# Depthwise convolution by token pairs in one step of a streaming encoder

## The chip, the cores and the metric

The kernel runs on one core of a Trainium2 chip. The metric is the device time of one execution in microseconds (us). The kernel before takes 1048.87 us (median of 3 runs, 1048.4 to 1048.88).

## The reference

One layer of a streaming encoder: 16 meta tokens and 1024 prompt frames of a new stream, and 32 frames of a running stream. One input projection feeds two head groups. Group A is a gated linear unit (GLU), then a causal depthwise convolution of width 31 over 512 channels, a LayerNorm over the channels and a swish. Group B is sliding-window attention with sinks. Both go through one output projection; a convolutional feed-forward and norms follow.

```python
def conv_module(glu_ext, dw_w, dw_b, ln_g, ln_b):
    y = depthwise_causal_conv(glu_ext, dw_w, dw_b)      # y[t] = b + sum_k w[k] * glu_ext[t + k], k = 0..30
    return jax.nn.silu(layernorm(y, ln_g, ln_b))
...
        a_out = conv_module(glu_ext, conv_dw_w[l], conv_dw_b[l], conv_ln_g[l], conv_ln_b[l])
        attn = prompt_attention(q, k, v, rel_bias_table, attn_sinks[l])
        xp = xp + jnp.concatenate([a_out, attn], axis=-1) @ w_out[l]
        xp, ffn_state = conv_ffn(xp, ..., norm_ffn[l], w_up[l], ffn_dw_w[l], ffn_dw_b[l], w_down[l])
```

## The kernel before

Channels lie on the 128 partitions, tokens along the free dimension. Tokens come in three blocks of 336, 384 and 352 (`TB`). Every product of large matrices is three matmuls of rounded parts: each operand is split into a high part (a cast on ScalarE, ACT) and a low part (a subtraction on VectorE, DVE, or a negated copy on ScalarE plus an accumulating DMA on GpSimd's queue, POOL). `mm3` (L252) issues the three: high by high (L255), high by low (L256), low by high (L257). TensorE is PE in the profile.

The stages, in order of time: the input projection (to about 164 us, the last two of its columns within attention), attention (164 to 248 us), the output projection, first its attention half (248 to 293 us, tiles `cah`, `cal`), then its convolution half (from 293 us, tiles `cvh`, `cvl`), and the feed-forward (to 990 us and beyond).

The convolution is done on VectorE, one instruction per tap and piece (`conv_taps`, L395; taps at L400 for the first and L403 for the rest): `acc = glu * w + acc`, with one weight per partition. There are four blocks of 128 channels, p = 0 to 3. `SEGS` (L84) says in which pieces of tokens a block is done: block 0 in two, of which 20 taps of the long one are done by ScalarE and accumulating DMAs (`chain_taps`, L414); blocks 1 and 2 in one piece of 1090 columns; block 3 in three pieces of 324, 384 and 382. A piece can begin when the GLU of its last token block is there. Taps wait in a queue (`tapq`) as chains. `taps(us)` (L437) takes taps from the first two chains in turn until a budget is spent, counting (n + 120) / 960 us for n columns; they are given a very low priority.

The order on TensorE and ScalarE is written out by hand in this part (`manual_schedule`, L709): these engines run in program order. VectorE's, SyncE's and GpSimd's orders are fixed when the program is built, by a simulated time line, in which a ready instruction of higher priority goes first.

Attention is a loop of 20 steps (L1007). Step i does the scores, the row maximum (here a minimum of negated scores, L757, DVE) and the exponentials (L764, ACT) of job i; the scaling by the reciprocal of the sum and the transposes (L821, L823, PE; copied out at L828, ACT) of job i - 1; and the product with the values (L837, L841, PE) and its copy (L845, ACT) for job i - 2. `SCA[i]` (L73) is how many of up to four scalings ScalarE does (L774); VectorE does the rest (L772). Between, `FILL[i]` (L76) rows of the last two input columns give TensorE work until step 11; from step 13 `AH` (L86) rows of the output projection do. `TA[i]` (L55) is the budget of taps. `ca_split` (L931) splits the attention output; the parts named in `CSD` (L85) have their low part made by ScalarE and a DMA, the others by VectorE (L250).

After attention come 20 groups of the attention half, four rows of three matmuls each (L1118). Each row is followed by a `tick` (L1095), so there are 80 ticks. Ticks drive three LayerNorms (`ln`, L1050), one per token block: the first begins at tick `LN0` = 14, each next one at least `LNS` ticks later, and only when all taps of its token block are issued (`any(t[0] <= b for t in tapq)`). Within one, `LNW` (L67) spaces the parts: sums, mean on TensorE (L1059) and its subtraction (L1061), squares (L1065, L1067), the sum of squares on TensorE (L271), which stands 4 + 3 + 9 = 16 ticks after the beginning, the scale (L286, L292, L1077), the swish (L1080), and last the split into `cvh` and `cvl` (L249, L250). That split needs its buffers, which `open_cv` (L1108) opens in the place of the GLU once the sums of squares of all three are issued; the test stands at the end of a group (L1134). Ahead of each token block of the convolution half, what is left of its LayerNorm is run off, in program order.

The weights of the convolution half are four tiles, used in the order `WOC` = (0, 2, 1, 3), each for two of eight output rows i (`conv_half`, L1155). The first is split within the attention half, the other three right after it, one after the other (L1141): a cast on ScalarE (L240), a subtraction on VectorE (L242), then `fetch` starts the next load. Two load buffers (`raw`) are there, so that the fourth tile's load waits for the second's split.

Of the kernel before, what the change touches and what calls it, by code (L numbers as in the profile page):

```python
# [18 lines left out]
P = 128  # L19
# [32 lines left out]
NPB = 8  # L52
TGS = [3.0, 3.0, 1000.0, 1000.0]
TGW = [3.0, 5.0, 6.5, 3.5, 1000.0, 1000.0, 5.0, 1000.0, 1000.0, 1000.0, 3.5, 3.5, 1000.0, 1000.0, 1000.0, 1000.0, 1000.0, 1000.0, 3.0, 3.0, 1000.0, 1000.0, 1000.0, 1000.0, 1000.0, 1000.0, 7.0, 3.5, 3.5, 3.5]
TA = [2.01, 2.74, 5.63, 6.64, 4.22, 3.28, 2.42, 2.68, 2.08, 1.57, 2.08, 2.08, 3.18, 1.41, 2.1, 0.85, 4.71, 3.21, 5.98, 2.57]  # L55
TH = 5.9
WAYS = 2
BS = ((0, 2), (1, 0), (2, 1), (2, 2))
# [11 lines left out]
WLD = True  # L70
MANUAL = {mybir.EngineType.PE, mybir.EngineType.Activation}
MANEND = MANUAL | {mybir.EngineType.DVE}
SCA = [1, 2, 2, 2, 1, 1, 2, 2, 2, 2, 2, 1, 2, 2, 0, 1, 1, 2, 2, 2]  # L73
LN0 = 14
LNS = 21
FILL = [4, 6, 6, 2, 3, 3, 6, 1, 3, 3, 1, 4, 5, 0, 3, 6, 0, 3, 0, 3]  # L76
ORDER = [2, 3, 8, 9, 4, 5, 10, 11, 12, 13, 6, 7]
CHAINS = ((0, 1),)
# [2 lines left out]
CHK = 21  # L81
CHT = 0
CHG = (1, 2)
SEGS = (((0,), (1, 2)), ((0, 1, 2),), ((0, 1, 2),), ((0,), (1,), (2,)))  # L84
CSD = ['12', '00']  # L85
AH = (1, 2, 1, 3, 5, 4, 5)  # L86
AG = (('00', '02'), ('h',), ('l',), ('10',), ('12',))
AT = (1, 8)
# [81 lines left out]
def body(nc, tc, cp, wp, xp, dp, io):  # L170
# [221 lines left out]

    tapq, spare = [], [0.0, 0]

    def conv_taps(p, a0, a1, b):  # L395
        e, a = glu[:, p, :], acc[:, p, a0:a1]

        def tap(k):
            if k == 0:
                nc.vector.tensor_scalar(out=a, in0=e[:, a0:a1], scalar1=pcol("cw", p * CW), scalar2=pcol("cb", p),  # L400
                                        op0=ALU.mult, op1=ALU.add)
            else:
                nc.vector.scalar_tensor_tensor(out=a, in0=e[:, a0 + k:a1 + k], scalar=pcol("cw", p * CW + k),  # L403
                                               in1=a, op0=ALU.mult, op1=ALU.add)

        ks = list(range(CW))
        if (p, b) in CHAINS:
            ks = [0, *range(CHK, CW)]
            chq.append([p, a0, a1, list(range(1, CHK))])
        tapq.append([b, a1 - a0, tap, ks, p])  # L410
# [288 lines left out]
    def fetch():  # L699
        if wsrc:  # L700
            raws.append(wraw(wsrc.pop(0)))
# [434 lines left out]
    if not CVH:  # L1136
# [1 line left out]
        while len(squared) < 3:  # L1138
            tick()
        open_cv()  # L1140
    for m2 in WOC[1:]:  # L1141
        whl[m2] = halves(take((None, None, *wres)[m2], WLD))
        fetch()

    close(cS)
    cH, ph = pool("h3", "right")
# [8 lines left out]
    def conv_half(b, rms):  # L1155
        t0, n = OB[b]
        at = t0 - H0
        for i, m in enumerate(2 * h + j for h in WOC for j in range(2)):
            hi, lo = whl[m // 2][m % 2]
            ps = mmt()[:, :n]  # L1160
            for k in range(4):
# [736 lines left out]
```

## Time and profile before

| what | value |
| --- | --- |
| median of 3 runs | 1048.87 us |
| the profiled execution | 1049.94 us |
| its span, first to last instruction | 1048.2 us |
| granted TensorE clock | 0.999 of full |
| TensorE busy | 1030.8 us (98%) |
| VectorE busy | 864.8 us (83%) |
| ScalarE busy | 506.6 us (48%) |
| DMA, mean | 119 GB/s |

A row of a group gives the line, the engine, the operation, what is written and read, the shape and the count, then the busy time in us and the mean of one in ns, then the engine's idle time ahead of them. A row of the time line or of the chain begins with its start and its length in us from the start of the span. A row of a stage gives its bounds and length, the busy time of PE, PEld (weight loading), DVE, ACT and POOL with the numbers of instructions, the granted clock, the share of the DMA engines and GB/s. [...]

### The profile page before, as it was taken

The numbers are of one execution on the slowest core, as the hardware profiler recorded it, in microseconds if no ns is written. First come the engines' busy times: TensorE is split into PE (matmuls) and PEld (weight loads), VectorE is DVE, ScalarE is ACT, GpSimd is POOL, SyncE is SP. The second block draws the span as 40 slices with busy tenths as digits, with TensorE's granted clock in tenths as the row PEclk, the third lists the DMA queues.
The fourth block names the chain that finished last, engine by engine and source line by source line (L and its number), as shares of the span: only waits on it lengthen the run. The fifth ranks groups of instructions, "written<-read, shape, count | busy, mean of one in ns | idle before, by whom it ended". The sixth has DMA issues, their size and how long they took to land.

```text
span 1048.2 us, 19994 instructions
## 1 busy us (share of the span) xinstructions
PE 1030.8 (98%) x7747; PEld 1004.9 (96%) x7747; DVE 864.8 (83%) x1649; ACT 506.6 (48%) x1074; POOL 163.0 (16%) x205
## 2 busy tenths in 40 slices
PE   9999999989999999999999999999999999999997
PEld 8999998758999999999999999999999999999997
DVE  7999988899978978888887888888777976986636
ACT  8653336896676744433333443343336722532334
POOL 1133220002325220001000000110010041000043
PEclk9999999999999999999999999999999999999999
DMA  7378673124963123243233233332426795832204
GB/s 268 90 170 163 146 152 81 41 54 70 174 151 108 61 71 102 72 141 96 72 110 125 63 103 109 97 103 76 130 63 207 250 194 132 249 123 69 94 2 166
DMA packets 69047, 124.41 MB, mean 119 GB/s; under 512 B 10448, under 2 KB 42568, under 8 KB 68952
## 3 DMA queue, kind: packets, MB, share of 16 engines
q1 hardware_dynamic: 56392, 97.77, 29.2%
q0 software_dynamic: 12128, 24.95, 14.1%
q8 instruction: 61, 1.00, 0.4%
q10 hardware_dynamic: 432, 0.41, 0.1%
q14 instruction: 34, 0.28, 0.1%
HBM read 79.42 MB, written 27.51 MB: 102 GB/s over the span
## 4 chain that ended last, share of the span: by engine, by line
PE 88%; ACT 6%; DVE 3%; DMA 2%; issue 1%; DVEq 0%; ACTq 0%
PE mm L1282 55%; PE mm L255 10%; PE mm L256 10%; PE mm L257 10%; ACT pb L764 1%; DVE acc L403 1%; ACT glu L828 1%; DMA raw<-woc 1%; PE R L292 1%; ACT hi L341 1%; PE R L271 1%; DMA xs<-xT 0%; ACT glu L764 0%; ACT pb L774 0%; DMA prm<-prm 0%
## 5 line engine op out<-in xcount | busy, mean ns | idle before, releaser
L1282 PE MATMUL mm<-bh,sl 128*128 128x264 f32 (+1 forms) x912 | 214.0, 284 | 0.0
L1282 PEld LDWEIGHTS mm<-bh,sl 128*128 128x128 f32 x912 | 157.2, 188 | 0.0
L403 DVE SCALAR_TENSOR_TENSOR acc<-glu,prm,acc 128x324 f32<-128x324 f32 (+4 forms) x190 | 155.0, 844 | 1.1
L1282 PE MATMUL mm<-bl,sl 128*128 128x264 f32 (+1 forms) x424 | 120.9, 285 | 0.0
L1282 PE MATMUL mm<-th,rawr 128*128 128x264 f32 x640 | 120.0, 284 | 0.0
L1282 PE MATMUL mm<-bh,wlo 128*128 128x264 f32 (+1 forms) x440 | 117.6, 284 | 0.0
L1424 DVE TENSOR_TENSOR x<-x,mm 128x264 f32<-128x264 f32 (+7 forms) x238 | 76.5, 347 | 45.6 <-PE mm L1282 45.4
L1282 PE MATMUL mm<-bh,whi 128*128 128x264 f32 (+1 forms) x440 | 112.5, 284 | 0.0
L255 PE MATMUL mm<-hi,whi 128*128 128x352 f32 (+3 forms) x312 | 104.0, 333 | 0.0
L256 PE MATMUL mm<-lo,whi 128*128 128x352 f32 (+3 forms) x312 | 101.2, 324 | 0.2 <-DVE lo L342 0.2
L257 PE MATMUL mm<-hi,wlo 128*128 128x352 f32 (+3 forms) x312 | 101.2, 324 | 0.0
L1282 PEld LDWEIGHTS mm<-th,rawr 128*128 128x128 f32 x640 | 100.4, 188 | 0.0
L1282 PE MATMUL mm<-th,sl 128*128 128x264 f32 x352 | 92.7, 284 | 0.0
L1282 PE MATMUL mm<-tl,rawr 128*128 128x264 f32 x320 | 90.8, 284 | 0.0
L1282 PEld LDWEIGHTS mm<-bh,wlo 128*128 128x128 f32 x440 | 80.6, 188 | 0.0
L1282 PEld LDWEIGHTS mm<-bl,sl 128*128 128x128 f32 x424 | 79.9, 188 | 0.0
L1282 PEld LDWEIGHTS mm<-bh,whi 128*128 128x128 f32 x440 | 79.0, 188 | 0.0
L1282 PE MATMUL mm<-bl,whi 128*128 128x264 f32 (+1 forms) x272 | 77.5, 285 | 0.0
L1218 ACT CAST sl<-x 128x512 fp32r<-128x512 f32 (+1 forms) x41 | 29.7, 727 | 74.2 <-DMA x<-wup 41.0
L1282 PEld LDWEIGHTS mm<-th,sl 128*128 128x128 f32 x352 | 63.8, 188 | 0.0
L1282 PEld LDWEIGHTS mm<-tl,rawr 128*128 128x128 f32 x320 | 60.3, 188 | 0.0
L255 PEld LDWEIGHTS mm<-hi,whi 128*128 128x128 f32 x312 | 58.7, 188 | 1.2 <-issue 0.6
(400 smaller groups left out, 2923.1 us busy)
## 6 DMA issues: line engine op xcount, KB each, us to landing
x<-wup SPq DMA_DIRECT2D x20, 512.0 KB, 4.3
x<-wup SPq DMA_DIRECT2D x40, 256.0 KB, 2.8
yq<-x SPq DMA_DIRECT2D x32, 264.0 KB, 2.8
wlo<-raw POOLq DMA_DIRECT2D x16, 512.0 KB, 4.6
ca<-ca POOLq DMA_DIRECT2D x18, 383.0 KB, 5.2
raw<-win SPq DMA_DIRECT2D x12, 512.0 KB, 4.5
raw<-wdn SPq DMA_DIRECT2D x12, 512.0 KB, 4.6
rb<-yq SPq DMA_DIRECT2D x10, 528.0 KB, 5.0
```

Source lines behind the costliest of these rows:

```text
L255: nc.tensor.matmul(ps, whi(k), xhi(k), start=first and i == 0, stop=False)
L256: nc.tensor.matmul(ps, whi(k), xlo(k), start=False, stop=False)
L257: nc.tensor.matmul(ps, wlo(k), xhi(k), start=False, stop=last and i == n - 1)
L271: nc.tensor.matmul(ss[:, i:i + 1], z[:, at:at + P], ones[:, 0:1], start=j == 0, stop=j == len(parts) - 1)
L292: nc.tensor.matmul(R[:, at:at + P], left[i], diag[i], start=True, stop=True)
L341: hid[b, k] = nc.scalar.activation(HI[b][:, k, :], X[b][:, k, :], AF.Copy, scale=pcol("g1", k)).ins
L403: nc.vector.scalar_tensor_tensor(out=a, in0=e[:, a0 + k:a1 + k], scalar=pcol("cw", p * CW + k), in1=a, op0=ALU.mult, op1=ALU.add)
L764: nc.scalar.activation(qs_[i], qs_[i], AF.Exp, bias=m[0][:, i:i + 1], scale=-1.0, accum_out=m[1][:, i:i + 1])
L828: nc.scalar.copy(ptb[kv], pts[kv])
L1218: nc.scalar.copy(hi, raw)
L1282: nc.tensor.matmul(ps, w[:, j, :], x[:, j, :], start=first and j + i == 0, stop=j == 3 and i == 2, skip_group_check=True)
L1424: summed[0] = nc.vector.tensor_tensor(out=z, in0=z, in1=ps[:, lo_:hi_], op=ALU.add).ins
```

## The change

Block 1 and block 2 (whole) and block 3 (its two later token blocks as one piece now) are convolved by pairs of neighbouring output columns. With `y0`, `y1` the even and odd outputs, e(k) every second input from k on, and w the 31 weights, the sums e(1) + e(2) are made once (one instruction of n + 14 columns, kept where acc of block 3 or glu of block 2 is free). Fifteen taps with the odd weights go over shifted windows of these sums into `y1`, which then holds S = b + sum_j w[2j+1] (e(2j+1) + e(2j+2)). Then y0 = S + sum_j (w[2j] - w[2j-1]) e(2j) and y1 = S + sum_j (w[2j] - w[2j+1]) e(2j+1), sixteen taps each, in turn: three half sums of products where the direct form has four. So a piece of 2n columns takes 1 + 15 + 32 = 48 instructions of about n columns, where 31 of 2n columns stood. All operands but the sums are read and written at every second element. The weight differences are made once on GpSimd (`pdif`).

With it go: new budgets `TA` for steps 7 to 19 (fewer taps in 12 to 17); one scaling fewer on ScalarE in steps 12, 13 and 16 (`SCA`); no part of the attention output split by ScalarE and DMA (`CSD` empty), so that VectorE subtracts; `LNS` 24 for 21; and the fourth weight tile of the convolution half is split ahead of row 4 of the first token block instead of right behind the third's.

```diff
-TA = [2.01, 2.74, 5.63, 6.64, 4.22, 3.28, 2.42, 2.68, 2.08, 1.57, 2.08, 2.08, 3.18, 1.41, 2.1, 0.85, 4.71, 3.21, 5.98, 2.57]
+TA = [2.01, 2.74, 5.63, 6.64, 4.22, 3.28, 2.42, 2.7, 2.5, 2.3, 2.4, 2.4, 1.9, 0.9, 0.9, 0.9, 0.9, 0.9, 3.0, 3.0]
...
-SCA = [1, 2, 2, 2, 1, 1, 2, 2, 2, 2, 2, 1, 2, 2, 0, 1, 1, 2, 2, 2]
+SCA = [1, 2, 2, 2, 1, 1, 2, 2, 2, 2, 2, 1, 1, 1, 0, 1, 0, 1, 2, 2]
 LN0 = 14
-LNS = 21
+LNS = 24
...
-SEGS = (((0,), (1, 2)), ((0, 1, 2),), ((0, 1, 2),), ((0,), (1,), (2,)))
-CSD = ['12', '00']
+SEGS = (((0,), (1, 2)), ((0, 1, 2),), ((0, 1, 2),), ((0,), (1, 2)))
+PAIRS = ((1, 0), (2, 0), (3, 1))
+NP2 = CW // 2
+CSD = []
...
+    pdif = cp.tile([P, NCV - 1, 2, NP2], F32, tag="pdif", name="pdif")
+    co = PRM["cw"][0] + CW
+    wv = prm[:, co:co + (NCV - 1) * CW].rearrange("p (a b) -> p a b", b=CW)
+    nc.gpsimd.tensor_tensor(out=pdif[:, :, 0], in0=wv[:, :, 2::2], in1=wv[:, :, 1::2], op=ALU.subtract)
+    nc.gpsimd.tensor_tensor(out=pdif[:, :, 1], in0=wv[:, :, 0:CW - 1:2], in1=wv[:, :, 1::2], op=ALU.subtract)
+
+    def pair_place(p, n):
+        return (None, acc[:, 3, ACCW - n:], acc[:, 3, 0:n], glu[:, 2, 0:n])[p]
+
+    def pair_taps(p, a0, a1, b):
+        n = (a1 - a0) // 2
+        sums = pair_place(p, n + NP2 - 1)
+        y = [acc[:, p, a0 + i:a1:2] for i in range(2)]
+
+        def e(k, m=n):
+            return glu[:, p, a0 + k:a0 + k + 2 * m - 1:2]
+
+        def one(out, x, w, into):
+            nc.vector.scalar_tensor_tensor(out=out, in0=x, scalar=w, in1=into, op0=ALU.mult, op1=ALU.add)
+
+        def tap(k):
+            i, j = k
+            if i == 0:
...
+                nc.vector.tensor_tensor(out=sums, in0=e(1, m), in1=e(2, m), op=ALU.add)
+            elif i == 1:
+                w, x = pcol("cw", p * CW + 2 * j + 1), sums[:, j:j + n]
+                if j == 0:
+                    nc.vector.tensor_scalar(out=y[1], in0=x, scalar1=w, scalar2=pcol("cb", p), op0=ALU.mult,
+                                            op1=ALU.add)
+                else:
+                    one(y[1], x, w, y[1])
+            elif i == 2:
+                w = pcol("cw", p * CW) if j == 0 else pdif[:, p - 1, 0, j - 1:j]
+                one(y[0], e(2 * j), w, y[0] if j else y[1])
+            else:
+                w = pdif[:, p - 1, 1, j:j + 1] if j < NP2 else pcol("cw", p * CW + CW - 1)
+                one(y[1], e(2 * j + 1), w, y[1])
+
+        ks = [(0, 0), *((1, j) for j in range(NP2)), *((i, j) for j in range(NP2 + 1) for i in (2, 3))]
+        tapq.append([b, n, tap, ks, p])
+
     def conv_taps(p, a0, a1, b):
+        if (p, b) in PAIRS:
+            pair_taps(p, a0, a1, b)
+            return
...
-    for m2 in WOC[1:]:
+    def conv_weights(m2):
         whl[m2] = halves(take((None, None, *wres)[m2], WLD))
         fetch()
+
+    for m2 in WOC[1:3]:
+        conv_weights(m2)
...
         for i, m in enumerate(2 * h + j for h in WOC for j in range(2)):
+            if b == 0 and i == 4:
+                conv_weights(WOC[3])
```

More of the change, by code (lines that the diff above doesn't have):

```diff
@@ L393, in body @@
     tapq, spare = [], [0.0, 0]
+    pdif = cp.tile([P, NCV - 1, 2, NP2], F32, tag="pdif", name="pdif")
[16 more added lines that the diff above has]
+            if i == 0:
+                assert not any(q[4] == p - 1 and (p == 3 or len(q[3]) > 2 * (NP2 + 1)) for q in tapq if q[2] is not tap)
+                m = n + NP2 - 1
+                nc.vector.tensor_tensor(out=sums, in0=e(1, m), in1=e(2, m), op=ALU.add)
[14 more added lines that the diff above has]
+        tapq.append([b, n, tap, ks, p])
     def conv_taps(p, a0, a1, b):
+        if (p, b) in PAIRS:
+            pair_taps(p, a0, a1, b)
+            return
         e, a = glu[:, p, :], acc[:, p, a0:a1]
```

## The prediction

> **What bounds the kernel now.** I read the page first, then the busy time by stage, then TensorE's waits.
>
> ```profile
> span 1048.2 us, 19994 instructions
> PE 1030.8 (98%) x7747; PEld 1004.9 (96%) x7747; DVE 864.8 (83%) x1649; ACT 506.6 (48%) x1074; POOL 163.0 (16%) x205
> ```
>
> TensorE is the bound of the whole; a shorter vector program is worth only what TensorE idles for. The stages (start:end, length, busy time of PE, PEld, DVE, ACT, POOL) say where it idles. The input projection is the first row, attention steps 0 to 5 the second, steps 6 to 11 the third, 12 to 17 the fourth; then come the attention half of the output projection and, from 293 us, its convolution half.
>
> ```profile
> 42.00:164.00 122.00, 121.94 (x759) 119.27 (x757) 114.42 (x165) 50.47 (x86) 29.66 (x42) 1.00 0.71 149
> ...
> 164.00:193.00 29.00, 27.42 (x201) 22.23 (x199) 22.73 (x90) 23.91 (x82) 0.85 (x1) 1.00 0.26 60
> 193.00:216.00 23.00, 22.24 (x166) 16.82 (x166) 22.67 (x83) 19.05 (x65) 0.00 (x0) 1.00 0.05 19
> 216.00:244.00 28.00, 23.44 (x176) 16.44 (x178) 27.81 (x103) 27.38 (x88) 3.31 (x3) 1.00 0.34 65
> 244.00:294.00 50.00, 50.00 (x319) 48.14 (x314) 43.44 (x97) 33.32 (x72) 18.35 (x17) 1.00 0.73 127
> 294.00:312.00 18.00, 16.05 (x106) 15.55 (x105) 13.64 (x23) 11.13 (x23) 4.10 (x5) 1.00 0.66 180
> 312.00:990.00 678.00, 678.00 (x5456) 677.92 (x5455) 557.38 (x927) 284.89 (x538) 79.67 (x100) 1.00 0.39 117
> ```
>
> TensorE idles 1.58, 0.76 and 4.56 us in the attention stretches, and 1.95 from 294 us: 8.85 us, the most that this change can win. Its waits in steps 0 to 5, in steps 12 to 17 and from 294 us (engine, line, releaser: total, times, longest):
>
> ```profile
> PE pt L821 <- DVE glu L772: 1.0, 1, 1.0
> ...
> PE o L837 <- ACT ca L845: 2.2, 5, 0.8
> PE pt L821 <- ACT pb L774: 1.3, 2, 0.9
> PE o L902 <- ACT ca L845: 0.8, 1, 0.8
> ...
> PE mm L255 <- DVE x L1165: 1.9, 2, 1.7
> ```
>
> In steps 12 to 17 the releaser is ScalarE, and both ScalarE (27.38 of 28) and VectorE (27.81) are full. In steps 6 to 11 VectorE is full (22.67 of 23) and ScalarE is not, while TensorE has only 0.76 us to spare.
>
> **The pair arithmetic.** What one tap costs (line, engine, shapes, count, busy time, mean ns), and how close taps follow each other in the time line (start, length of the run):
>
> ```profile
> L403 DVE SCALAR_TENSOR_TENSOR acc<-glu,prm,acc 128x1090 f32<-128x1090 f32 x60 | 80.3, 1348 | 0.6
> L403 DVE SCALAR_TENSOR_TENSOR acc<-glu,prm,acc 128x324 f32<-128x324 f32 x55 | 30.1, 547 | 0.2
> L400 DVE TENSOR_SCALAR acc<-glu,prm 128x1090 f32<-128x1090 f32 x2 | 1.7, 841 | 0.0
> ...
> 193.66 2.33 DVE L403 SCALAR_TENSOR_TENSOR acc<-glu,prm,acc 128x324 f32<-128x324 f32 x4
> 244.34 4.83 DVE L403 SCALAR_TENSOR_TENSOR acc<-glu,prm,acc 128x384 f32<-128x384 f32 x9
> ```
>
> The first two rows give a line: (1348 - 547) / (1090 - 324) = 1.05 ns per element, so 778 ns at 545 elements and 609 at 383. Nine taps of alternating chains take 4.83 us, 0.54 each, 0.07 less than one alone: taps overlap by that much. So a tap takes 1.27 us at 1090, 0.70 at 545, 0.53 at 383, 0.47 at 324. Four taps of one chain on the same accumulator take 2.33, 0.58 each: a tap that needs the one before it costs 0.1 more.
>
> A channel block of 1090 columns costs 30 x 1.27 + 0.77 = 38.9 us now, and as pairs 48 instructions of 0.70, 33.6: 5.3 us less for each of blocks 1 and 2. Block 3's two long pieces cost 62 x 0.53 = 32.9 now and 48 x 0.53 = 25.4 as one pair: 7.5 less. Three sums for four save 18 us of VectorE, not a quarter of it, since 48 short instructions pay the fixed part where 31 paid it. The two weight differences are 45 elements each on POOL, which is idle for most of the span (163.0 us busy); I put them at nothing, since block 1's first tap, the first that could wait for them, is late enough (63.98 us, a row below).
>
> No instruction of this trace reads every second element, so 0.70 is an assumption: bounds are 0.70 (as 545 adjacent elements) and 1.27 (as if all 1090 were passed over). I take 0.70, because the instruction still reads and writes 545 elements.
>
> [...]
>
> **Steps 0 to 5.** Block 2's taps run into attention now:
>
> ```profile
> 63.98 0.84 DVE L400 TENSOR_SCALAR acc<-glu,prm 128x1090 f32<-128x1090 f32 x1
> ...
> 113.35 0.84 DVE L400 TENSOR_SCALAR acc<-glu,prm 128x1090 f32<-128x1090 f32 x1
> ...
> 165.19 1.34 DVE L403 SCALAR_TENSOR_TENSOR acc<-glu,prm,acc 128x1090 f32<-128x1090 f32 x1
> ...
> 173.74 1.34 DVE L403 SCALAR_TENSOR_TENSOR acc<-glu,prm,acc 128x1090 f32<-128x1090 f32 x1
> ```
>
> Blocks 1 and 2 begin at 63.98 and 113.35; the last two rows are the first and last of the five long taps after 164 us (6.4 us). VectorE is 114.42 of 122 us full before that, so of both savings (10.6 us) at least 7 arrive at the end of block 2, and the five vanish. The one wait on VectorE (L772, 1.0 us) goes: **-1.0 us** (0 if the pairs are late, -1.2 with its restart). The other waits there are ScalarE's and stay.
>
> **Steps 6 to 11.** Block 3's long piece can begin only when its last columns are there (the 216.12 row), so here only its first piece, 324 wide, runs, as one chain. The budgets of steps 7 to 11 rise from 10.49 to 12.3 us. Counting as the code does (444/960 us a tap of 324), 27 taps are issued in steps 6 to 11 before and 32 after. What ran:
>
> ```profile
> 216.12 0.55 DVE L582 SCALAR_TENSOR_TENSOR glu<-mm,glu 128x320 f32<-128x320 f32 x2
> ...
> L403 DVE SCALAR_TENSOR_TENSOR acc<-glu,prm,acc 128x324 f32<-128x324 f32 x18 | 9.9, 549 | 0.2
> L403 DVE SCALAR_TENSOR_TENSOR acc<-glu,prm,acc 128x384 f32<-128x384 f32 x7 | 4.3, 612 | 0.0
> ```
>
> These 25 and two first taps are the 27. Five more add 5 x 0.47 = 2.4; seven narrower ones take off 0.4; about half of them wait for their predecessor, +0.7. Of 2.7 us, TensorE's slack takes about 0.8: **+1.9 us** (0 if taps find gaps, +2.7 if no slack).
>
> **Steps 12 to 17.** Budgets fall from 15.46 to 6.4 us. VectorE gains three softmax scalings and four subtractions, ScalarE loses three scalings and four negated copies:
>
> ```profile
> L774 ACT ACTIVATE pb<-pb,sm 128x209 f32<-128x209 f32 x14 | 6.4, 487 | 0.0
> ...
> L936 ACT ACTIVATE cal<-ca 128x384 fp32r<-128x384 f32 x2 | 1.1, 560 | 0.0
> ...
> L936 ACT ACTIVATE cal<-ca 128x324 fp32r<-128x324 f32 x2 | 1.0, 476 | 0.0
> ...
> L772 DVE TENSOR_SCALAR pb<-pb,sm 128x209 f32<-128x209 f32 x10 | 3.0, 321 | 0.0
> ...
> L250 DVE TENSOR_TENSOR cvl<-acc,cvh 128x324 fp32r<-128x324 f32 x4 | 1.8, 490 | 0.0
> ```
>
> VectorE's balance is some -9.1 + 3 x 0.24 + 4 x 0.42 = -6.7 us (the last row is a subtraction of the same kind); ScalarE's 3 x 0.37 + 2 x 0.38 + 2 x 0.42 = 2.7 (each 0.1 less than its busy time, for overlap). With VectorE no longer full, ScalarE is the bound, and I take what it loses: **-2.6 us**; ends 0 and -4.6, all of TensorE's idle time there. The two accumulating transfers on POOL's queue go with the copies; nothing behind them was late.
>
> **The weights and the normalisation.** With a spacing (LNS) of 24 the three LayerNorms begin at ticks 14, 38, 62 (a tick is one row of three matmuls, four to a group, 80 in all), not 14, 35, 56. The third has its squares summed 16 ticks after it begins: tick 78, not 72. Only at the end of that group are the split buffers opened: before, two groups were left; now none.
>
> ```profile
> 288.56 0.72 PE L271 MATMUL S<-ones,glu 128*128 128x1 f32 x6
> ...
> 293.06 0.31 PE L255 MATMUL mm<-cvh,whi 128*128 128x324 f32 x1
> ...
> 289.99 1.55 ACT L249 CAST cvh<-acc 128x324 fp32r<-128x324 f32 x4
> ...
> 293.61 1.05 ACT L240 CAST wrh<-raw 128x1024 fp32r<-128x1024 f32 x1
> 294.56 1.05 ACT L240 CAST whi<-raw 128x1024 fp32r<-128x1024 f32 x1
> 302.48 1.05 ACT L240 CAST wrh<-raw 128x1024 fp32r<-128x1024 f32 x1 [6.87 <-DMA raw<-woc]
> ...
> 294.69 1.23 DVE L242 TENSOR_TENSOR wrl<-raw,wrh 128x1024 fp32r<-128x1024 f32 x1 [2.06 <-ACT wrh L240]
> ```
>
> The 289.99 row, which hid behind the last two groups, now stands in ScalarE's written order behind the two weight casts (293.61, 294.56), while TensorE wants its result at 293.06. Its first cast ends near 295.5 + 0.4. VectorE then has both weight subtractions (1.23 each, from 294.7, until 297.0) and the first split's (0.4): TensorE resumes at 297.3, **+4.2 us**. If VectorE takes the split's subtraction before the second weight's, it is 3.1; nothing else is left for TensorE to do.
>
> In return the third cast waited 6.87 us for its load with everything of ScalarE's behind it, and TensorE waited 1.9 for that (L1165 above). Behind row four ScalarE reaches it near 306, when the load has landed: **-1.9 us**. Its subtraction ends near 308, when row six asks for it at 308.0: **+0.2** (0 to 0.6).
>
> **Sum.** -1.0 + 1.9 - 2.6 + 4.2 - 1.9 + 0.2 = +0.8 us. The profiled execution took 1049.94 us (span 1048.2 and 1.7 around it), so 1050.7 by it; that execution is 1.07 above the median 1048.87, so I predict 1049.7 against the median.
>
> **Rivals.**
>
> *VectorE is the bound all through (faster).* It has no gap from 193 to 244 us. If its lighter load reaches TensorE wholly and the extra taps find gaps: -1.0 + 0 - 4.6 + 2.5 = -3.1, 1045.8. For it: 27.81 of 28. Against: ScalarE's 27.38 beside it, and the waits name ScalarE. 0.27.
>
> *The long pair holds the second LayerNorm (slower).* Before, that LayerNorm needed only the middle piece of block 3; now all 48 instructions.
>
> ```profile
> 248.48 0.37 PE mm L255
> ...
> 269.37 0.65 PE S L1059 x2
> ```
>
> The second row of the chain is the second mean now, 20.9 us after the first matmul behind attention; three ticks later it stands at 22.4. By the budgets 23 pair instructions (12.2 us) are left after attention, and 17 passes of 0.4 to 0.5 us (four subtractions, the first LayerNorm, the second's sums), 8 us, stand ahead of that mean. The margin is some 2 us; every us beyond by which VectorE leaves attention late is a us of wait. A run like that at 244.34, 4.83 us behind, would cost 2.8: +3.6, 1052.5. For it: VectorE is 9 tenths full there (43.44 of 50). Against: it leaves steps 12 to 17 less loaded. 0.2.
>
> *Every second element costs double (slower).* Then 48 x 1.27 = 61 us for 38.9, twice, and 48 x 0.93 for 32.9: +56 us, of which VectorE's free time before attention and after it takes some 15: near 1090. For it no row, against it none. 0.04.
>
> **The numbers.** My forecast has 0.49. What counts as a change of this kernel is 0.2%, 2.1 us. The forecast's own ends are 1046.5 and 1052; with the two middle rivals the range is 1045.2 to 1053. Faster 0.29 (the first rival and the forecast's lower edge), same 0.45, slower 0.26.
>
> **What would show it.** Tap rows of 545 near 0.78 us busy (1.35 would be the last rival). No wait on L772 near 171 us. TensorE idle above 2 us in steps 6 to 11 and near 2 in steps 12 to 17; if the latter falls under 0.5, VectorE was the bound. A TensorE wait of 3 to 4.4 us ahead of the first cvh matmul, released by VectorE's cvl (L250), with no wait on L1165 later: its absence would prove the last part wrong. A wait on the second L1059 would be the slower rival.

## The result and the profile after

The changed kernel takes 1057.18 us (median of 6, 1056.23 to 1057.86) beside 1049.41 for the kernel before (median of 6 on the same chip): a ratio of 1.0073, 95% interval 1.006 to 1.0086, so 7.7 us slower. The forecast was 1049.7, within 1045.2 to 1053. Three executions of the later runs that took far longer (1295.03, 1683.14 and 4186.4 us) are in no ratio. The two profiled executions differ by less than the medians, 6.9 us, as the one before (1049.94) lies 0.5 us above its median here and the one after (1056.83) 0.35 below. In this part a number in us for a run is its ratio less one, times the median of the kernel before.

The line numbers of the changed kernel are shifted: the three matmuls are L257 to L259, the weight cast L242 and its subtraction L244, the cast and subtraction into `cvh` and `cvl` L251 and L252, VectorE's scaling L820, the pair taps L415, the direct taps L451. First the head of the page after.

```profile
span 1055.1 us, 20008 instructions
...
PE 1035.5 (98%) x7747; PEld 1009.0 (96%) x7747; DVE 849.3 (80%) x1677; ACT 504.6 (48%) x1066; POOL 159.8 (15%) x205
```

VectorE is 15.5 us less busy (864.8 before) and the span is 6.9 us longer. The groups of the pair taps by shape say that the saving is what the arithmetic promised:

```profile
L415 DVE SCALAR_TENSOR_TENSOR acc<-glu,pdif,acc 128x545 f32<-128x545 f32 x60 | 43.2, 781 | 0.0
...
L415 DVE SCALAR_TENSOR_TENSOR acc<-glu,pdif,acc 128x383 f32<-128x383 f32 x30 | 16.6, 609 | 0.0
```

The prediction had 778 and 609 ns. So reading and writing every second element costs nothing that these two rows show.

Two of the same stretches, steps 12 to 17 and the beginning of the convolution half (the columns are start:end, length, busy PE, PEld, DVE, ACT, POOL, granted clock, DMA share, GB/s):

```profile
216.00:244.00 28.00, 23.42 (x168) 17.15 (x168) 26.45 (x99) 24.15 (x77) 0.86 (x1) 0.94 0.18 40
...
294.00:312.00 18.00, 14.14 (x79) 13.52 (x78) 13.31 (x27) 10.78 (x23) 3.86 (x6) 0.81 0.46 125
```

In both the granted clock is below 1, where before it was 1.00 in every stretch. In the second, TensorE is 14.14 us busy with 79 matmuls, before 16.05 with 106: fewer matmuls, each longer. TensorE's waits (engine, line, releaser: total, times, longest):

```profile
PE o L885 <- ACT ca L893: 3.9, 7, 1.3
PE mm L257 <- ACT cvh L251: 2.8, 1, 2.8
PE pt L940 <- DVE pb L820: 2.1, 1, 2.1
...
PE mm L258 <- DVE cvl L252: 0.9, 1, 0.9
PE mm L259 <- DVE wrl L244: 0.8, 1, 0.8
PE mm L257 <- ACT wrh L242: 0.4, 1, 0.4
```

The wait on L772 (1.0) is gone, and so are those at the old L1165 (1.9). New are 2.8 and 0.9 at the first split, 0.8 and 0.4 for the fourth weight tile, and 2.1 in attention. These are the engines around the first split, one fence each for ScalarE, VectorE and TensorE (rows of neighbours overlap a little, as 294.39 + 1.05 and 295.33 do):

```profile
294.39 1.05 ACT L242 CAST wrh<-raw 128x1024 fp32r<-128x1024 f32 x1
295.33 1.05 ACT L242 CAST whi<-raw 128x1024 fp32r<-128x1024 f32 x1
296.28 1.55 ACT L251 CAST cvh<-acc 128x324 fp32r<-128x324 f32 x4
```

```profile
295.47 1.23 DVE L244 TENSOR_TENSOR wrl<-raw,wrh 128x1024 fp32r<-128x1024 f32 x1 [0.79 <-ACT wrh L242]
296.61 1.22 DVE L244 TENSOR_TENSOR wlo<-raw,whi 128x1024 fp32r<-128x1024 f32 x1
297.75 1.71 DVE L252 TENSOR_TENSOR cvl<-acc,cvh 128x324 fp32r<-128x324 f32 x4
```

```profile
296.80 0.64 PE L257 MATMUL mm<-cvh,whi 128*128 128x324 f32 x1 [2.79 <-ACT cvh L251]
298.29 0.64 PE L258 MATMUL mm<-cvl,whi 128*128 128x324 f32 x1 [0.86 <-DVE cvl L252]
...
299.53 0.47 PE L259 MATMUL mm<-cvh,wlo 128*128 128x324 f32 x1
299.80 0.47 PE L257 MATMUL mm<-cvh,whi 128*128 128x324 f32 x1
...
303.23 0.31 PE L259 MATMUL mm<-cvh,wlo 128*128 128x324 f32 x1
303.38 0.31 PE L257 MATMUL mm<-cvh,whi 128*128 128x324 f32 x1
```

Two weight casts, then the four casts of the split; two weight subtractions, then the split's: the order that the prediction wrote down. But from 298.7 to 302.8 the matmuls are 0.27 us apart, and only then 0.15: half speed through the first output row (twelve matmuls) and into the second.

The same matmuls can be compared start by start. TensorE is later than before by 0.5 us ahead of the old wait on L772 and 0.6 *earlier* behind it; 1.5 earlier at 217.5; 0.3 later at 223.1; 1.8 later at 235.5; 0.7 later at the end of the attention half. Then 5.1 at the first cvl matmul (293.21 before, 298.29 after), 7.2 where full speed is back, 5.9 where the old wait stood, 6.6 behind the fourth tile's split, and 6.9 near the end. So the 6.9 us are 0.7 up to the convolution half, 4.4 of waits at the first split, 2.1 of slow rows, and -0.3 from there on.

### The profile page after: what moved, and what is told of

Read it like the earlier page. It is cut to its first block, busy times and chain, and to the rows that moved or that the text cites. A ratio compares the mean times of both kernels' runs of the same rounds, so it can differ in the third digit from the quotient of the medians.

```text
span 1055.1 us, 20008 instructions
## 1 busy us (share of the span) xinstructions
PE 1035.5 (98%) x7747; PEld 1009.0 (96%) x7747; DVE 849.3 (80%) x1677; ACT 504.6 (48%) x1066; POOL 159.8 (15%) x205
## 4 chain that ended last, share of the span: by engine, by line
PE 89%; DVE 5%; ACT 4%; DMA 1%; issue 1%; DVEq 0%; ACTq 0%
PE mm L1335 54%; PE mm L257 10%; PE mm L258 10%; PE mm L259 10%; ACT pb L812 1%; DVE acc L451 1%; PE R L294 1%; ACT hi L343 1%; ACT glu L876 1%; PE R L273 1%; DMA xs<-xT 1%; DVE acc L415 0%; ACT glu L812 0%; DMA prm<-prm 0%; PE vt L725 0%
## 5 line engine op out<-in xcount | busy, mean ns | idle before, releaser
L257 PE MATMUL mm<-hi,whi 128*128 128x352 f32 (+3 forms) x312 | 104.0, 333 | 0.0
L259 PE MATMUL mm<-hi,wlo 128*128 128x352 f32 (+3 forms) x312 | 101.2, 324 | 0.0
L415 DVE SCALAR_TENSOR_TENSOR acc<-glu,pdif,acc 128x545 f32<-128x545 f32 (+1 forms) x90 | 59.9, 724 | 0.0
L257 PEld LDWEIGHTS mm<-hi,whi 128*128 128x128 f32 x312 | 58.7, 188 | 1.0 <-issue 0.6
```

Source lines behind the costliest of these rows:

```text
L257: nc.tensor.matmul(ps, whi(k), xhi(k), start=first and i == 0, stop=False)
L259: nc.tensor.matmul(ps, wlo(k), xhi(k), start=False, stop=last and i == n - 1)
L415: nc.vector.scalar_tensor_tensor(out=out, in0=x, scalar=w, in1=into, op0=ALU.mult, op1=ALU.add)
```

## The experiments

The theory after this reading: two stalls (first split, attention) cost time by themselves and a second time by the clock; the pairs are innocent and useless. The rivals: the vector engine's new program is the cause in both places, or the stalls only move.

**The first split, by the tick.**

```diff
-LNS = 24
+LNS = 22
```

> The changed kernel with LNS 22 for 24: the third LayerNorm begins at tick 58, its squares are summed at tick 74, and the split buffers open one group before the end of the attention half, so that the first token block's four cvh casts stand ahead of the two weight casts. Theory (the order behind the two weight casts is the cause, and the idle time also halves the granted clock for 6.8 us): the waits of 2.79 and 0.86 us ahead of the first cvh matmuls go, the granted clock stays full at 296 to 303 us, and the time falls from 7.8 us over the kernel before to about +0.8 (5.1 of the arrival of the first low part, 1.9 of the clock), between -0.5 and +2. Rival (the vector engine is late there in any case, with the third LayerNorm or the weights' low parts): a wait of 2 to 4 us stays at the first two rows under another name, and the time at +4 to +7.

Measured 1.0059, 1.0047 to 1.0072: +6.2, where +0.8 was expected. The first split's waits did go: the first cvl matmul is at 294.13, 4.2 us earlier. But a new one took their place, on the fourth weight tile (ScalarE, then TensorE):

```profile
305.45 2.48 ACT L1128 ACTIVATE acc<-acc,prm 128x382 f32<-128x382 f32 x4
...
308.65 1.03 ACT L242 CAST wrh<-raw 128x1024 fp32r<-128x1024 f32 x1
```

```profile
309.73 0.64 PE L257 MATMUL mm<-cvh,wrh 128*128 128x324 f32 x1 [3.11 <-ACT wrh L242]
310.99 0.64 PE L259 MATMUL mm<-cvh,wrl 128*128 128x324 f32 x1 [0.35 <-DVE wrl L244]
```

The cast has no wait for its load any more. It comes late because it stands behind the third block's swish (L1128) and the squares and high parts of the rows before it, which wait for VectorE. And behind this wait the clock is halved in its turn: 0.64 where 0.41 would stand, and matmuls 0.27 us apart (311.43, 311.70, 311.97) where they were 0.15 apart ahead of the wait. So the theory fell in its simple form: the late first split had *hidden* a second fault.

**The first split, by the order alone.**

```diff
+    for _ in lns[0]:
+        pass
     for m2 in WOC[1:3]:
         conv_weights(m2)
```

> The changed kernel with what is left of the first token block's LayerNorm (its four casts and subtractions into cvh and cvl) written ahead of the second and third weight tile's splits; LNS stays 24. Theory (only the place in ScalarE's and the vector engine's order matters, not the tick): the first cvh cast runs at 294.4 us instead of 296.3, TensorE idles 0.8 and 0.3 us instead of 2.79 and 0.86, too little to lose the clock: 4.9 us below the changed kernel, +2.9 over the kernel before (+2 to +4); with a clock loss all the same, +4.8. Rival (the weights' low parts then come late instead): +5 to +8, with a wait on the second tile's low part (L244) ahead of row two.

Measured 1.0045, 1.0032 to 1.0059: +4.7, some 3 us better than the change, 1.8 more than the +2.9 that was expected. The cvh cast runs at 294.17, TensorE waits 0.9 there instead of 2.8 and 0.9. The rest went where it went in the run before: 1.8 and 0.7 us of waits for the fourth tile. So it is the order on ScalarE and VectorE (the edit moves casts and subtractions together), not the tick, that made the stall; neither repair pays while the fourth tile stands where the change put it.

**The clock, parted from the wait.** Two runs give TensorE idle work in the wait, products that nothing reads; the output is the same.

```diff
             ps = mmt()[:, :n]
+            for _ in range(20 if b == 0 and i == 0 else 0):
+                nc.tensor.matmul(ps[:, :256], hi[:, 0, :], hi[:, 0:2, :]..., start=True, stop=True)
```

> The changed kernel with 20 matmuls of 256 columns added ahead of the first row of the convolution half, into the same PSUM tile, whose first product then overwrites them (about 2.4 us of work that needs no split; they add nothing to the result). The wait for the first cvh stays as long, TensorE only isn't idle in it. Theory (idle time of 2.79 us halves the granted clock, which costs 1.9 us of its own on top of the wait): no halved clock at 296 to 303 us, matmuls of 324 columns 0.15 us apart there, time 1.9 us below the changed kernel: +5.9 over the kernel before (5.2 to 6.4). Rival (the rows are slow there because they wait, and the clock has no part in it): +7.8, with the first rows as far apart as before; if the added matmuls outlast the wait, more.

Measured 1.006, 1.0048 to 1.0073: +6.3, 1.4 below the change, in the stated direction, though the two intervals overlap; half of the slow stretch was left, as the second wait, ahead of the first cvl matmul, was still idle. So the run was made complete, with 22 such matmuls in the first wait and 9 in the second:

```diff
+                if b == 0 and i == 0 and k == 0:
+                    fill(22)
+                    nc.tensor.matmul(ps, hi[:, 0, :], CVH[b][:, 0, :], start=True, stop=False)
+                    fill(9)
+                    nc.tensor.matmul(ps, hi[:, 0, :], CVL[b][:, 0, :], start=False, stop=False)
...
```

> The changed kernel with TensorE kept busy in both waits of the first split: 22 matmuls of 256 columns ahead of the first cvh matmul and 9 between it and the first cvl matmul, all into a PSUM tile of their own that nothing reads (0.12 us each by the earlier run: 2.6 and 1.1 us for waits of 2.79 and 0.86 and the matmuls' own latency). Theory (the halved clock costs 1.9 us on top of the waits): no halved clock from 290 to 310 us, 1.9 us below the changed kernel, +5.9 over the kernel before (+5.3 to +6.5). Rival (the rows only run into the fourth tile's split earlier): its wait ahead of row six grows from 1.2 to about 3 us and the time stays at +7.3 to +7.8.

Measured 1.0053, 1.0041 to 1.0066: +5.6, 2.1 below the change. TensorE's time line in this run:

```profile
293.74 2.78 PE L1218 MATMUL mm<-whi 128*128 128x256 f32 x22
296.70 0.42 PE L1223 MATMUL mm<-cvh,whi 128*128 128x324 f32 x1 [0.18 <-ACT cvh L251]
296.96 1.23 PE L1218 MATMUL mm<-whi 128*128 128x256 f32 x9
298.19 0.42 PE L1225 MATMUL mm<-cvl,whi 128*128 128x324 f32 x1
298.45 0.31 PE L1226 MATMUL mm<-cvh,wlo 128*128 128x324 f32 x1
298.59 0.31 PE L257 MATMUL mm<-cvh,whi 128*128 128x324 f32 x1
```

The first cvl matmul starts at 298.19 as it did at 298.29 in the changed kernel, so the wait is as long as it was; but behind it the matmuls are 0.15 apart at once. The two intervals just overlap, but the starts of the matmuls say the same as the times: where the changed kernel is 7.2 us later than the kernel before (at full speed again), this run is 5.1 later, and near the end 4.8 against 6.9. That parts the two: the wait is 4.4 us, the clock 2.1 more.

**Each late part alone, in the kernel before.** First the spacing.

```diff
-LNS = 21
+LNS = 24
```

> The kernel before with LNS 24 alone (the fourth weight tile in its old place, right behind the third). Theory: the first token block's four cvh casts now stand behind three weight casts, of which the last waits for its load until 302.5 us; the first cvh then comes at 303.9, TensorE idles from 293.1 to 304, then 1.0 more for the low part, and loses the clock for 6.8 us or more; the old waits of 1.9 at 304 go: +11 us (+9 to +14). Rival (the place in ScalarE's order costs little by itself, and the changed kernel's waits at 296 us come with the pairs): +0 to +3.

Measured 1.0105, 1.0092 to 1.0119: +11.0, as expected. TensorE's wait:

```profile
PE mm L255 <- ACT cvh L249: 9.1, 1, 9.1
```

Without a single pair, the spacing alone makes the stall, and a far longer one, because the last of three weight casts, which waits for its load, also stands ahead of the split. This frees the pairs from blame, and says what moving the fourth tile did in the change: it kept the damage of LNS 24 to 4.4 us.

Then the fourth tile. (Of this kernel two runs stand here; TensorE's waits are those of the second.)

```diff
-    for m2 in WOC[1:]:
...
+    for m2 in WOC[1:3]:
...
+            if b == 0 and i == 4:
+                conv_weights(WOC[3])
```

> The kernel before with one part of the change alone: the fourth weight tile split ahead of row four instead of right behind the third (LNS stays 21). The prediction's step: ScalarE no longer waits 6.87 us for that load with everything of its own behind it, TensorE's 1.9 us of waits at 304 us go: -1.7 (with 0.2 for a late low part; -2.3 to -1.3). Theory now, from the run with LNS 22: the cast stands behind the squares and high parts of rows one to three in ScalarE's order, and these wait for the vector engine, which has the second block's low parts and the third block's normalisation ahead of them; so the cast comes at about 308 us where row six asks for it at 305, TensorE waits some 3 us for it (L240) and loses the clock for 6.8 us: +3 to +5.5. If the clock holds, +1 to +2.

> The kernel before with the fourth weight tile ahead of row four alone, for a profile at full clock (the earlier one stood at a granted clock of 0.73 all through). It took +1.6. Theory: the waits of 1.9 at 304 us are gone and a wait on that tile's cast or low part (L240, L242) of 1.5 to 2.5 us stands ahead of row six, with the clock halved for one window of 3.4 us, 1.7 us of work. If no clock is lost, a wait of 3.5 us.

Measured 1.0015 (1.0006 to 1.0024) and 1.0011 (1.0002 to 1.002): +1.6 and +1.2. The forecast of -1.7 in the prediction is refuted. ScalarE and TensorE in the second run:

```profile
304.18 1.03 ACT L240 CAST wrh<-raw 128x1024 fp32r<-128x1024 f32 x1
```

```profile
305.26 0.41 PE L255 MATMUL mm<-cvh,wrh 128*128 128x324 f32 x1 [0.77 <-ACT wrh L240]
306.68 0.41 PE L257 MATMUL mm<-cvh,wrl 128*128 128x324 f32 x1 [0.85 <-DVE wrl L242]
```

Waits of 1.62 us for the tile's cast and low part took the place of 1.9 for its load, so this profiled execution (1050.05 us, clock 0.999) stands where that of the kernel before stands (1049.94). But the latter was one of its longer ones. Of the 11 executions here, five at a granted clock of 0.999 took 1049.98 to 1050.28; twelve of the kernel before at 0.999 on the same chip have a median of 1049.10. So some 0.9 us is lost at full clock already. The other six, at 0.996 to 0.998, took 1050.90 to 1051.59. The expectation that one clock window is lost in every execution was wrong: the one with a trace has a granted clock of 1.00 from 290 to 312 us. That about half of them lose one is an estimate from the granted clocks above: 3.41 us at half clock are 0.0016 of a span of 1048.3.

Last, the same tile two rows earlier:

```diff
...
+            if b == 0 and i == 2:
+                conv_weights(WOC[3])
```

> The kernel before with the fourth weight tile ahead of row two alone. Theory (place decides: behind the second block's casts, ahead of the rows that wait for the vector engine): -1.0 against the kernel before (-1.9 to -0.5), waits at 304 us under 0.5. Rival (the gain of the run with row two came from the pairs' lighter vector load): +0 to +1.5.

Measured 1047.87 us, 0.9986, 0.9977 to 0.9995: 1.5 us *faster* than the kernel before. ScalarE:

```profile
299.35 0.55 ACT L303 ACTIVATE bh<-x,prm 128x324 fp32r<-128x324 f32 x1
301.27 1.05 ACT L240 CAST wrh<-raw 128x1024 fp32r<-128x1024 f32 x1 [1.37 <-DMA raw<-woc]
302.23 2.50 ACT L1080 ACTIVATE acc<-acc,prm 128x382 f32<-128x382 f32 x4
```

The cast now waits 1.37 us for its load instead of 6.87, ahead of the swish and of the rows that wait for VectorE, and TensorE has no wait left from 294 to 312 us.

**The changed kernel with the old spacing.**

```diff
-LNS = 24
+LNS = 21
```

> The changed kernel with LNS 21, the fourth weight tile still split ahead of row four. Theory (two causes that can be added: the spacing, which is undone here, and the tile's place, which cost 1.6 us by itself in the kernel before; the pairs and attention cost 0.6): +2.2 over the kernel before (+1.5 to +3.2), a wait of some 2 us for the fourth tile (L242 or L244) ahead of row six, and no loss of the clock there. Rival (with LNS 22 the same place cost 5.8 over the run with both parts undone; if that is due to the pairs' load and not to the extra group): +5 to +6.5, with the clock halved near 306.

Measured 1.003, 1.0019 to 1.0042: +3.1, at the upper edge. Its waits for the fourth tile are 0.8 and 0.8 us, shorter than expected, but the clock is halved once there (below); both theories were half right.

**Pairs and attention.** First everything but the two late parts (LNS 21, the fourth tile in its old place), then only the pairs, with all budgets and scalings of before:

```diff
-LNS = 24
+LNS = 21
...
-    for m2 in WOC[1:3]:
+    for m2 in WOC[1:]:
...
-            if b == 0 and i == 4:
-                conv_weights(WOC[3])
```

> The changed kernel with the two last parts undone: LNS 21, and the fourth weight tile split right behind the third. The pairs and all edits of attention stay (tap budgets, scalings, no accumulating transfers). Theory (these parts together leave TensorE 0.2 to 0.7 us later when attention and the attention half are over, the rest of the loss is the end): the old waits of 1.9 at 304 us are back, the time is +0.5 over the kernel before (0 to +1.2). Rival (the load of the pairs on the vector engine also delays the convolution half): +2 or more, with new waits behind 293 us.

> The kernel before with the pairs alone: new pieces and pair taps, all budgets, scalings, accumulating transfers, LNS and weight splits as before the change. Theory (18 us less of vector time, of which the path sees only the one wait on L772 at 171 us): -1.2 us, between -2 and 0, no wait of 2 us at 223, full clock from start to end. If the freed vector time reaches TensorE in steps 12 to 17 after all, -3 to -5. Rival (the long pair, which must be whole ahead of the second LayerNorm, holds it): a wait on the second mean (L1107), +1 to +4.

Measured 1.0006 (0.9997 to 1.0015) and 1.0005 (0.9996 to 1.0014): no difference that can be told, for either. Of the run with the pairs alone:

```profile
PE 1031.5 (98%) x7747; PEld 1005.8 (96%) x7747; DVE 849.3 (81%) x1669; ACT 507.2 (48%) x1074; POOL 161.4 (15%) x207
```

VectorE's 15.5 us are gone here too, and the time is that of before: the convolution by pairs costs and gains nothing that this run resolves. TensorE gains 1.1 us at the old L772 wait, of which 0.4 had been lost ahead of it; 0.5 are still there at 293 us, and near the end it is 0.3 later than in the kernel before, for a reason that no run shows.

Then the 2.1 us wait at 223 us, first in the changed kernel, then without its late parts:

```diff
-SCA = [1, 2, 2, 2, 1, 1, 2, 2, 2, 2, 2, 1, 1, 1, 0, 1, 0, 1, 2, 2]
+SCA = [1, 2, 2, 2, 1, 1, 2, 2, 2, 2, 2, 1, 1, 2, 0, 1, 0, 1, 2, 2]
```

> The changed kernel with two scalings on ScalarE in step 13 (SCA[13] = 2, as before the change), all else as changed. Theory (the 2.1 us wait of the transposes at 223 us comes from a scaling that stands behind four row maxima on the vector engine, and halves the granted clock for 3.4 us; but TensorE waits for ScalarE anyway in these steps, so it is recouped by 240 us): wait and clock loss are gone, the time falls by 0.3 to 0.8 us only, to about +7.2 over the kernel before. Rival (the stall and the lost clock reach the end): 2.1 and some 1.3 us fewer, +4.4.

> The run with pairs and attention edits alone (LNS 21, fourth tile in its old place), with two scalings on ScalarE in step 13 again. Theory (the 2.1 us wait at 223 us and the clock it halves are the one cost of the attention edits, worth some 1.5 to 1.9 us at the end): +0.6 - 1.6 = -1.0 against the kernel before (-1.9 to -0.3). Rival (recouped by 240 us, as TensorE waits for ScalarE there in any case): +0.6.

Measured 1.0058 (1.0045 to 1.007), so 1.6 below the change, and 0.9996 (0.9987 to 1.0005), 1.0 below the run it stems from. The wait of 2.1 is gone; about half of wait and clock loss reaches the end, more than the first theory's 0.3 to 0.8. Neither difference is clear of its intervals by itself, but the matmuls' starts agree: with step 13 put back the run without the late parts is 1.6 us earlier at 248 us and 1.4 near the end. The clock was halved once all the same, by two waits of 0.76 and 0.92 us (below). With all scalings of before:

```diff
-SCA = [1, 2, 2, 2, 1, 1, 2, 2, 2, 2, 2, 1, 1, 1, 0, 1, 0, 1, 2, 2]
+SCA = [1, 2, 2, 2, 1, 1, 2, 2, 2, 2, 2, 1, 2, 2, 0, 1, 1, 2, 2, 2]
```

> The run with pairs and attention edits alone, with all scalings (SCA) as before the change, so that steps 12, 13 and 16 have one more on ScalarE; tap budgets and the missing accumulating transfers stay. Theory (the scalings that went to the vector engine in steps 12 and 16 relieve ScalarE, which TensorE waits for): 0.3 to 0.8 worse than with step 13 alone put back, so -0.7 to +0.3 against the kernel before. Rival (VectorE is no longer free enough for any of them): equal or better than with step 13 alone, -1 to -1.8.

Measured 0.9999, 0.9991 to 1.0008: -0.1, not to be told from the run with step 13 alone. So lighter scalings on ScalarE in steps 12 and 16 are worth nothing measurable.

**A version that beats both.** The changed kernel with LNS 21, step 13 put back and the fourth tile ahead of row two; and the same with all scalings of before.

```diff
-LNS = 24
+LNS = 21
...
-            if b == 0 and i == 4:
+            if b == 0 and i == 2:
```

> The run with step 13 put back (LNS 21), and the fourth weight tile split ahead of row two: behind the second block's cvh casts, so that these no longer wait for its load as in the kernel before, and ahead of the rows whose squares wait for the vector engine. Theory: the cast comes at 302.5 with the load, its low part by 304.9, row six asks at about 304: TensorE waits some 0.5 to 1 us in place of 1.9: 1 us better than the run with step 13 put back, -2 against the kernel before (-3 to -1). Rival (the vector engine's order, which has the second block's low parts and the third block's normalisation ahead of that low part, makes it late at any place but the old one): +0 to +2, with a wait on L244 ahead of row six.

> Pairs, tap budgets and no accumulating transfers as in the change, all scalings (SCA) as before it, LNS 21, the fourth tile ahead of row two. Theory (full clock all through in the run with these scalings; the tile worth 1.4 us as with step 13 alone put back): -1.2 against the kernel before (-2.2 to -0.5), equal to the run with step 13 put back within 1 us.

Measured 1047.27 us, 0.9984 (0.9975 to 0.9992), and 1047.94, 0.9986 (0.9977 to 0.9995). Both beat both kernels; neither can be told from the kernel before with the tile alone moved to row two (0.9986). The gain is the tile's place; the pairs and the budgets add nothing that these runs resolve.

## Why the prediction was wrong

**Right.** The cost of a tap (0.70 taken, its busy time 778 against 781 ns); most of the 18 us of VectorE (15.5 by busy time); steps 0 to 5 (-1.0 predicted, -1.04 by the matmuls' starts); and the mechanism of the first split, with the order of the two casts and two subtractions ahead of it: +4.2 predicted, 4.4 found, and the run with LNS 24 alone shows the spacing as its cause. The slower rival did not come: the second mean has no wait. Nor did the last rival.

**The term that was missing: the clock, 2.1 us.** No term of the sum held it. Every stretch of before had 1.00, and the 1.68 us wait at 304 us left it so; the prediction treated a wait as costing its length. The run that filled the waits measures it: the same wait, and an end 2.1 us earlier.

**Steps 6 to 11: +1.9 predicted, +0.2 found.** The step that failed is "Counting as the code does ... 32 after": a larger budget was taken for more work done there. The direct taps (L403 before, L451 after) in that stretch, first of the kernel before, then of the changed one:

```profile
193.00:216.00 23.00, 13.41 (x25) 1.00 0.05 19
```

```profile
193.00:216.00 23.00, 13.74 (x25) 1.00 0.03 10
```

25 taps ran in both. The budget only puts taps into the program at very low priority, and VectorE was full already (22.67 and 22.48 of 23 us); the last five taps of the changed kernel's chain ran after 216 us. A budget is a bound on what may be issued, not a measure of what runs.

**Steps 12 to 17: -2.6 predicted, +1.0 found.** TensorE is 0.5 us ahead of the kernel before when they begin, 1.5 ahead at 217.5, 0.3 behind at 223.1 and 0.5 behind at 244. ScalarE's relief did come. TensorE's waits for ScalarE in this stretch were 4.5 us before (1.5 of them for scalings, the `pb` rows), and after they are one group:

```profile
PE o L885 <- ACT ca L893: 2.5, 3, 1.3
```

The step that failed is "With VectorE no longer full, ScalarE is the bound, and I take what it loses". VectorE's part was counted as balance ("+ 3 x 0.24"), by its length and not by its order, so that the sum has no term for a wait on VectorE. (ScalarE's loss is 2.8 and not 2.7 by the prediction's own rows.) What ate the gain is one scaling (VectorE, then TensorE):

```profile
220.46 0.16 DVE L817 RECIPROCAL sm<-sm 128x2 f32<-128x2 f32 x1
220.53 0.36 DVE L805 CUSTOM_DVE_ANT_0 pb<-S,bt 128x209 f32<-128x209 f32 x1
...
221.70 0.56 DVE L451 SCALAR_TENSOR_TENSOR acc<-glu,prm,acc 128x324 f32<-128x324 f32 x1
222.17 0.62 DVE L415 SCALAR_TENSOR_TENSOR acc<-glu,prm,acc 128x383 f32<-128x383 f32 x1
222.70 0.31 DVE L820 TENSOR_SCALAR pb<-pb,sm 128x177 f32<-128x177 f32 x1
```

```profile
223.07 0.33 PE L940 MATMUL pt<-ident,pb 128*128 128x128 f32 x1 [2.10 <-DVE pb L820]
```

The scaling of 0.31 us has its reciprocal at 220.6 and then stands behind the next job's four row minima (220.53 to 221.70) and two taps, 1.2 and 1.0 us, and the transposes wait for it; the clock is halved behind that wait. With this scaling on ScalarE (the kernel before, and the runs with step 13 put back) these transposes waited 0.2. Putting this one back is worth 1.0 to 1.6 us at the end. Even then the run stands at 0.9996, 0.4 us below the kernel before and not to be told from it. TensorE's waits for ScalarE from 216 to 244 us are 2.0 in it, 2.5 us fewer than before, but a wait of 0.9 for VectorE's scalings (and one window at half clock) stands against them; with all scalings put back they are 2.8, and the wait for VectorE is 1.4. So the relief of ScalarE is real, and each time a part of it went into a wait for VectorE that the sum did not have. The faster rival falls with the run of the pairs alone: VectorE's lighter load did not reach the end.

**The fourth tile: -1.9 + 0.2 predicted, -0.5 found.** The old wait went (7.1 to 5.9 us late), 1.0 came back with waits of 0.4 and 0.8 for the tile's own cast and low part, and a last 0.3 went with the second of the old waits. The step that failed is "Behind row four ScalarE reaches it near 306": in the changed kernel the cast runs at 311.07, and in the kernel before with this part alone at 304.18, both times without a wait for its load. Ahead of it in ScalarE's order stand squares that wait for VectorE (3.47 and 1.87 us of such waits in the changed kernel, 0.79 in the other) and, in the other, the third block's swish (2.50 us). The prediction asked when the load would have landed, and not what else would stand ahead of the cast in ScalarE's order. By itself the part costs 1.2 to 1.6 us, and two rows earlier it gains 1.5. Also, the 1.9 was read off one execution, and a long one: its load came 8.9 us after the first weight cast and TensorE's first wait was 1.68 us. With the pairs alone both were much the same (8.9 and 1.75). In the three other traces with the tile in its old place (pairs and attention edits; the same with step 13 put back; with all scalings put back) the load came after 8.1, 8.2 and 7.7 us and the wait was 0.94, 1.01 and 0.49. So a usual execution of the kernel before may have less to win here, which no trace of it shows.

Against the sum of +0.8 the misses are 3.6 in steps 12 to 17, 2.1 for the clock, 1.2 for the fourth tile, 0.2 at the first split, 0.5 ahead of attention and 0.3 behind 310 us that no term held, and -1.7 in steps 6 to 11: the 6.9 us of the traces, but for rounding.

What stays open: the drift of 0.3 us between 310 us and the end, and why the pairs put TensorE 0.4 us behind ahead of 164 us, where VectorE is less busy. The tap budgets and the missing accumulating transfers were not run alone.

## What to carry to other kernels

A moved instruction cost here what stood ahead of it in its new queue, not its own length: the 1.03 us cast of the fourth tile ran at 311.07 us in the changed kernel, its load landed, behind squares that had waited 3.47 and 1.87 us for VectorE. For every move, list the queue at the new place and ask when each item there is ready. Before paying with other engines for a lighter engine, check that the bound engine waits for it: 15.5 us of VectorE bought nothing that can be told here, as TensorE's one long wait for it in attention was 1.0 us. And a stall of TensorE should be priced with its clock: behind one of 2.10 us the clock was halved here for 3.41 us, and two waits of together 3.65 us put TensorE 6.5 us back.

## What the hardware showed

In the trace of the changed kernel the clock is halved from 224.26, from 295.94 and from 1053.70 us on. The first two stretches are 3.41 and 6.83 us long, the last is cut off by the end of the span. The starts lie 71.68 and 757.76 us apart, 21 and 222 times 3.413, which fits a grid of 3.41 us that is fixed within the execution. In the kernel before the clock is halved only behind the last matmul, from 1046.44 us on. What goes with the halved stretches is how busy TensorE was in the window just before. Five windows of the changed kernel:

```profile
220.85:224.26 3.41, 1.31 (x11) 0.99 (x11) 3.41 (x15) 2.53 (x10) 0.00 (x0) 1.00 0.00 0
224.26:227.67 3.41, 3.41 (x20) 2.25 (x21) 3.38 (x11) 1.52 (x4) 0.86 (x1) 0.50 0.11 20
292.53:295.94 3.41, 1.47 (x10) 1.18 (x9) 1.13 (x5) 2.11 (x4) 2.07 (x3) 1.00 0.66 106
295.94:299.35 3.41, 1.70 (x5) 1.35 (x6) 3.41 (x6) 2.78 (x8) 0.08 (x1) 0.50 0.85 123
299.35:302.76 3.41, 3.41 (x14) 3.41 (x13) 0.59 (x2) 0.57 (x2) 0.00 (x0) 0.50 0.79 297
```

A window with 1.31 or 1.47 us of TensorE work is followed by one at half clock, and one that is full (224.26) by full clock again (1.00 from 227.68 to 231.08). In the changed kernel with step 13 put back, the waits there are 0.76 and 0.92 us, and the clock was halved too:

```profile
222.22:225.64 3.42, 1.75 (x18) 1.01 (x18) 3.42 (x15) 3.42 (x12) 0.55 (x1) 1.00 0.00 0
225.64:229.05 3.41, 3.41 (x14) 3.15 (x14) 3.24 (x11) 2.93 (x10) 0.30 (x1) 0.50 0.80 154
```

The old wait at 304 us in the kernel before left 2.25 us of work in its window, and the clock stayed full (1.00 from 305.75 to 309.16 too):

```profile
302.33:305.75 3.42, 2.25 (x16) 1.98 (x14) 2.19 (x4) 3.27 (x7) 0.00 (x0) 1.00 0.11 41
```

Between these lie windows of the same length, at full clock too, behind which either happened. Half clock followed 1.75 us (above) and 1.78 us (the changed kernel with LNS 21, 304.59). It did not follow 1.77 us near the end of the changed kernel (1046.87), 1.68 us in the run with the order alone (305.02; its matmuls from 310.04 on are 0.15 us apart) or 1.82 us in the run with the pairs alone (302.27; the granted clock of that execution is 0.999). All are about half a window. A window that is itself at half clock can be followed by another: the one at 295.94 above, with 1.70 us, was.

From the start of the span, a halved stretch begins at 224.26 us in the changed kernel, at 225.64 with step 13 put back and at 308.00 with LNS 21, that is 2.39, 0.36 and 0.80 us past a multiple of 3.413: the grid lies elsewhere in each of these three executions. So the same stall could fall into one window or be cut by two. That would explain why the kernel before with the fourth tile ahead of row four has two groups of times 1.1 us apart; it is not shown, as the lower group alone has a trace.

The gaps were short: a wait of 2.10 us was followed by half clock in the changed kernel, and so were two of 0.76 and 0.92 us in one window with step 13 put back.
